# Rotary embedding (NeoX) on one core: joining the f32 heads' transfer, limiting the queued loads, cutting the tables in two

## The chip, the core and the metric

The kernel runs on one core of a Trainium2 chip. The metric is device microseconds of one execution. A profiled execution gives a span, which is about 1.8 us shorter than the device time of the same execution. The TensorE clock is 1.00 in all records; TensorE does nothing here.

On one core "slow" only means over 1.5% above the fastest run of the same kernel. Verdicts use fast runs alone; where I use a slow profile I say so.

## The reference

```python
def reference(x, freqs, positions):            # x: 8 x 8 x 1024 x 64 f32
    half = x.shape[-1] // 2
    angles = np.outer(positions, freqs)
    cos, sin = np.cos(angles), np.sin(angles)
    x_first, x_second = x[:, :, :, :half], x[:, :, :, half:]
    out_first = x_first * cos - x_second * sin
    out_second = x_first * sin + x_second * cos
    return np.concatenate([out_first, out_second], axis=-1)
```

There are 64 heads of 256 KB. Each is read once and written once.

## The kernel before

GpSimd issues the bulk of the traffic, in transfers that convert f32 to bf16 on the way in and bf16 to f32 on the way out. 62 heads go that way, in eight groups; a partition holds 64 positions of one head, 16 KB in HBM and 8 KB in SBUF. Heads 0 and 1 go through SP in f32, so that the DMA engines have work before the first bulk load. VectorE does three operations for each group (product with sine, product with cosine, sum of the first swapped and the second).

```python
    def hbm_head(t, i):
        return bass.AP(tensor=t.tensor, offset=t.offset + i * head, ap=[[R * d, P], [1, R * d]])
    ...
    xf = singles.tile([P, edge, R, d], f32)            # R = 8: 2 KB a partition and head
    for i in range(edge):
        nc.sync.dma_start(out=xf[:, i], in_=hbm_head(x, i))
    nc.scalar.dma_start(out=pos_i..., in_=positions...)
    nc.scalar.dma_start(out=fr[0:P:8], in_=freqs[None, :].to_broadcast([P // 8, half]))
    xts = []
    for lo, n in groups:                               # 6 heads, then seven times 8
        xt = xpool.tile([P, run], bf16, name="xt")[:n * chunks]
        parts = 2 if lo == groups[-1][0] else 1
        for a in range(0, run, run // parts):
            b = a + run // parts
            nc.gpsimd.dma_start(out=xt[:, a:b], in_=hbm(x, lo, n, a, b))
        xts.append(xt)
    ...
    pool.keepalive_nop(ins=[pool.lower_ap(xts[-1][:, :run // 2])])   # stores only after the loads
```

## Time and profile before

| | before |
|---|---|
| device time, first three runs | 86.14 us median (85.05 to 87.10) |
| profiled run | 84.02 us, span 82.1 us |
| all loads landed / all stores landed | 42.1 / 81.2 us |
| VectorE's last operation ends | 76.8 us |

How GpSimd issues its loads, here from the timeline (start, time, instruction, count; in brackets the idle time before it and what ended it):

```profile
1.26 4.37 POOL L82 DMA_DIRECT2D xt<-in_x_dram  x8 [0.82 <-PEq L231]
8.28 0.53 POOL L82 DMA_DIRECT2D xt<-in_x_dram  x1 [2.65 <-DMA xt<-in_x_dram]
40.37 1.05 POOL L184 DMA_DIRECT2D out_dram<-ot  x2 [31.45 <-DMA xt<-in_x_dram]
```

Eight of the nine loads are issued by 5.6 us and the ninth when the first has landed; then GpSimd waits for the loads and begins with the stores. A transfer runs on 16 DMA engines and has landed only when the last has reported its share.

A transfer runs on 16 DMA engines, and each reports its own share; the trace holds the 16 moments for every transfer (no printed view of the profile shows them, and they do not say which engine reported). I give their median, the last (only then has the transfer landed), and the spread from first to last. In the profiled run before, the 16 engines land the first bulk load within 0.41 us of each other, and every later load within 0.41 us too. I call this "in step", and later also a profile in which no engine lands its share of the first load more than 0.5 us behind the median.

### The profile page before, as it was taken

To read this page: it belongs to the slowest core of one execution; us is meant where nothing else is said; L and a number is where in the kernel's file an instruction comes from. 1 tells how busy PE (TensorE), PEld (TensorE's weight loads), DVE (VectorE), ACT (ScalarE), POOL (GpSimd) and SP (SyncE) were. 2 spreads that over 40 slices of the span, in tenths; PEclk is the share of its full clock that TensorE was granted. 3 is DMA by queue.
4 is the path that set the end of the run, shared out by engine and by line. 5 is a ranking of instruction groups with operands and counts; after the bars stand their busy time and mean duration, and the time that the engine had idled before them with its cause. 6 is when DMAs were issued, how large, how long until landed. Compare 5 with 4: busy or idle time off the path is not lost.

```text
span 82.1 us, 157 instructions
## 1 busy us (share of the span) xinstructions
DVE 67.6 (82%) x49; ACT 9.4 (11%) x8; POOL 9.5 (12%) x22
## 2 busy tenths in 40 slices
DVE  0135996399999996999999999999999999999300
ACT  0600003999000007000000000000000000000000
POOL 4970300000000000000340020002002002002000
DMA  1999999999999999999999999999999999999992
GB/s 19 304 225 212 204 232 216 204 224 212 225 213 204 228 216 200 228 202 208 212 417 415 447 423 439 439 399 463 431 415 447 415 455 431 399 455 405 437 379 104
DMA packets 3456, 25.45 MB, mean 310 GB/s; under 512 B 560, under 2 KB 576, under 8 KB 1600
## 3 DMA queue, kind: packets, MB, share of 16 engines
q0 software_dynamic: 2384, 23.86, 95.0%
q1 hardware_dynamic: 864, 1.57, 5.6%
q10 hardware_dynamic: 208, 0.02, 0.3%
HBM read 16.80 MB, written 16.78 MB: 409 GB/s over the span
## 4 chain that ended last, share of the span: by engine, by line
DVE 78%; DMA 7%; ACT 4%; issue 4%; ACTq 1%
DVE t L151 22%; DVE ot L152 21%; DVE ot L154 19%; DMA const<-in_freqs_dram 7%; DVE turnsc L101 3%; DVE turnsc L95 3%; ACT sinc L105 2%; DVE wholec L99 2%; DVE of L168 2%; DVE of L171 1%; DVE last L154 1%; DVE last L152 1%; ACT cosr L109 1%; DVE sinc L106 1%; DVE turnsr L95 1%
## 5 line engine op out<-in xcount | busy, mean ns | idle before, releaser
L151 DVE TENSOR_TENSOR t<-xt,sinc 128x4096 bf16<-128x4096 bf16 (+3 forms) x9 | 18.3, 2046 | 0.0
L154 DVE TENSOR_TENSOR ot<-ot,t 128x4096 bf16<-128x4096 bf16 (+2 forms) x8 | 17.7, 2222 | 0.2
L152 DVE TENSOR_TENSOR ot<-xt,cosc 128x4096 bf16<-128x4096 bf16 (+2 forms) x8 | 17.6, 2216 | 0.0
L184 POOL DMA_DIRECT2D out_dram<-ot x8 | 4.2, 532 | 61.4 <-DMA xt<-in_x_dram 31.5
L82 POOL DMA_DIRECT2D xt<-in_x_dram x9 | 4.9, 573 | 3.5 <-DMA xt<-in_x_dram 2.6
L105 ACT ACTIVATE sinc<-turnsc 128x2048 bf16<-128x2048 f32 x1 | 1.9, 1909 | 10.3 <-DVE turnsc L101 10.3
L106 DVE TENSOR_SCALAR sinc<-sinc 128x2048 bf16<-128x2048 bf16 x1 | 0.7, 693 | 2.0 <-ACT sinc L105 2.0
L95 DVE TENSOR_TENSOR turnsc<-pos_f,fturn 128x2048 f32<-128x2048 f32 x1 | 2.3, 2291 | 0.0
L101 DVE TENSOR_TENSOR turnsc<-turnsc,wholec 128x2048 f32<-128x2048 f32 x1 | 2.3, 2291 | 0.0
L87 DVE LOAD_MASK_SELECT const<-const x1 | 0.0, 14 | 2.7 <-DMA const<-in_positions_dram 2.7
L109 ACT ACTIVATE cosc<-wholec,half_pi 128x2048 bf16<-128x2048 f32 x1 | 2.0, 2002 | 0.1
L88 DVE LOAD_MASK_SELECT const<-const x1 | 0.0, 14 | 2.3 <-DMA const<-in_freqs_dram 2.3
L108 ACT ACTIVATE wholec<-turnsc 128x2048 f32<-128x2048 f32 x1 | 1.9, 1893 | 0.0
L105 ACT ACTIVATE sinr<-turnsr 128x256 bf16<-128x256 f32 x1 | 0.4, 416 | 10.6 <-DVE turnsr L101 10.6
L105 ACT ACT_TABLE_LOAD x1 | 1.3, 1283 | 2.1 <-issue 2.1
L168 DVE TENSOR_TENSOR of<-x,cosr 128x1024 f32<-128x1024 bf16 x1 | 1.2, 1226 | 0.1
L99 DVE TENSOR_SCALAR wholec<-turnsc 128x2048 f32<-128x2048 f32 x1 | 1.2, 1228 | 0.0
L171 DVE TENSOR_TENSOR of<-of,t 128x1024 f32<-128x1024 f32 x1 | 1.2, 1225 | 0.0
L154 DVE TENSOR_TENSOR last<-last,t 128x1024 f32<-128x1024 f32 x1 | 1.2, 1224 | 0.0
L152 DVE TENSOR_TENSOR last<-xt,cosc 128x1024 f32<-128x1024 bf16 x1 | 1.2, 1218 | 0.0
L126 ACT CAST x<-xf 128x1024 bf16<-128x1024 f32 x1 | 1.0, 1028 | 0.0
L115 DVE CAST pos_f<-const 32x64 f32<-32x64 int32 x4 | 0.8, 211 | 0.1
(17 smaller groups left out, 4.7 us busy)
## 6 DMA issues: line engine op xcount, KB each, us to landing
out_dram<-ot POOLq DMA_DIRECT2D x6, 2048.0 KB, 11.1
xt<-in_x_dram POOLq DMA_DIRECT2D x6, 1024.0 KB, 21.8
out_dram<-ot POOLq DMA_DIRECT2D x2, 1536.0 KB, 6.3
xt<-in_x_dram POOLq DMA_DIRECT2D x2, 512.0 KB, 34.3
xt<-in_x_dram POOLq DMA_DIRECT2D x1, 768.0 KB, 6.7
xf<-in_x_dram SPq DMA_DIRECT2D x2, 256.0 KB, 2.9
out_dram<-of SPq DMA_DIRECT2D x2, 256.0 KB, 2.9
out_dram<-last SPq DMA_DIRECT2D x2, 256.0 KB, 4.0
```

The lines of the kernel that those rows point to most:

```text
L82: nc.gpsimd.dma_start(out=xt[:, a:b], in_=hbm(x, lo, n, a, b))
L95: pin(v.tensor_mul(out=turns, in0=pos_f.to_broadcast([P, n, half]), in1=fturn.to_broadcast([P, n, half])))
L99: pin(v.tensor_scalar(out=whole, in0=turns, scalar1=magic, scalar2=magic, op0=Alu.add, op1=Alu.subtract))
L101: pin(v.tensor_sub(out=turns, in0=turns, in1=whole))
L105: nc.scalar.activation(out=sin[:, :, 0], in_=turns, func=Act.Sin, scale=twopi)
L109: nc.scalar.activation(out=cos, in_=whole[:, :, None, :].to_broadcast([P, n, copies, half]), func=Act.Sin, scale=-twopi, bias=half_pi)
L151: pin(v.tensor_mul(out=t.rearrange(flat4), in0=xt, in1=sin_c[:n, lo:hi].rearrange(flat4)))
L152: pin(v.tensor_mul(out=ot, in0=xt.rearrange("p (c two h) -> p c two h", two=2, h=half), in1=cos_c[:n, lo:hi].to_broadcast([n, rows, 2, hal ...
L154: pin(v.tensor_add(out=ot, in0=ot, in1=swap(t)))
L168: pin(v.tensor_mul(out=o, in0=x0, in1=w.to_broadcast(flat)))
L171: pin(v.tensor_add(out=pair, in0=pair, in1=swap(t.rearrange(rows, two=2, h=half))))
L184: tc.keep_in_program_order(pool.dma_start(out=hbm(out, lo, n, 0, hi * d), in_=ot.rearrange(flat4)))
```

## The change

The intent: fewer and larger packets for the f32 heads, no long queue of loads in front of the small transfers, ScalarE and VectorE overlapped while the tables are made.

```diff
-    for i in range(edge):
-        nc.sync.dma_start(out=xf[:, i], in_=hbm_head(x, i))
+    nc.sync.dma_start(out=xf, in_=hbm_first(x))       # R = 16: 128 rows of 4 KB over both heads
...
     for lo, n in groups:
+        if len(xts) >= 2:
+            nc.gpsimd.keepalive_nop(ins=[nc.gpsimd.lower_ap(xts[-2])])
...
-        nc.scalar.activation(out=sin[:, :, 0], in_=turns, func=Act.Sin, scale=twopi)
+        for c in cuts:                                 # two halves for the large tables
+            pin(nc.scalar.activation(out=sin[:, c, 0], in_=turns[:, c], func=Act.Sin, scale=twopi))
...
-    tc.keep_in_program_order(nc.scalar.dma_start(out=pos_r...))
+    for i in range(edge):
+        pin(nc.scalar.dma_start(out=pos_r[i * each:(i + 1) * each]...))
...
-    for i in range(edge):
-        tc.keep_in_program_order(sp.dma_start(out=hbm_head(out, i), in_=of[:, i]))
+    tc.keep_in_program_order(sp.dma_start(out=hbm_first(out), in_=of.rearrange(flat4)))
```

Cut away: the VectorE operations are all pinned in order; the heads' tables are made between a group's cosine product and its sum; the signs of the sine table are set in halves; a small memset moves from GpSimd to VectorE.

More of the change, by code (lines that the diff above doesn't have):

```diff
@@ L36 @@
     C = 64
-    R = seq // P
     chunks = seq // C
@@ L40 @@
     edge = 2
+    R = edge * seq // P
     run = C * d
@@ L43 @@
     groups = [(edge, first)] + [(g, G) for g in range(G, bh, G)]
-    assert chunks * C == seq and G * chunks == P and bh % G == 0 and R * P == seq and chunks <= 32
+    assert chunks * C == seq and G * chunks == P and bh % G == 0 and R * P == edge * seq and chunks <= 32
     singles = ctx.enter_context(tc.tile_pool(name="singles", bufs=1))
@@ L53, in hbm, with hbm_first @@
                        ap=[[run, n * chunks], [1, b - a]])
-    def hbm_head(t, i):
-        return bass.AP(tensor=t.tensor, offset=t.offset + i * head, ap=[[R * d, P], [1, R * d]])
+    def hbm_first(t):
+        return bass.AP(tensor=t.tensor, offset=t.offset, ap=[[R * d, P], [1, R * d]])
     v = nc.vector
@@ L66 @@
     fr = const[:, C * words:].bitcast(f32)
-    xf = singles.tile([P, edge, R, d], f32)
-    for i in range(edge):
-        nc.sync.dma_start(out=xf[:, i], in_=hbm_head(x, i))
+    xf = singles.tile([P, R * d], f32)
+    nc.sync.dma_start(out=xf, in_=hbm_first(x))
     nc.scalar.dma_start(
@@ L73 @@
     nc.scalar.dma_start(out=fr[0:P:8], in_=freqs[None, :].to_broadcast([P // 8, half]))
+    half_pi = singles.tile([P, 1], f32)
+    v.memset(half_pi, math.pi / 2)
     xts = []
     for lo, n in groups:
+        if len(xts) >= 2:
+            nc.gpsimd.keepalive_nop(ins=[nc.gpsimd.lower_ap(xts[-2])])
         xt = xpool.tile([P, run], bf16, name="xt")[:n * chunks]
@@ L81 @@
             b = a + run // parts
-            nc.gpsimd.dma_start(out=xt[:, a:b], in_=hbm(x, lo, n, a, b))
+            tc.keep_in_program_order(nc.gpsimd.dma_start(out=xt[:, a:b], in_=hbm(x, lo, n, a, b)))
         xts.append(xt)
-    half_pi = singles.tile([P, 1], f32)
-    nc.gpsimd.memset(half_pi, math.pi / 2)
     v.stream_shuffle(pos_i, pos_i, [i % chunks for i in range(32)])
-    v.stream_shuffle(fr, fr, [0] * 32)
-    fturn = singles.tile([P, 1, half], f32)
-    v.tensor_scalar_mul(out=fturn[:, 0, :], in0=fr, scalar1=1.0 / twopi)
@@ L92, in tables @@
-    def tables(pos_f, n, copies, name, pin=lambda i: i):
+    pin = tc.keep_in_program_order
+    def tables(pos_f, n, copies, name, parts):
         turns = singles.tile([P, n, half], f32, name=f"turns{name}")
-        pin(v.tensor_mul(out=turns, in0=pos_f.to_broadcast([P, n, half]),
-                         in1=fturn.to_broadcast([P, n, half])))
         whole = singles.tile([P, n, half], f32, name=f"whole{name}")
-        magic = 1.5 * 2.0 ** 23
-        pin(v.tensor_scalar(out=whole, in0=turns, scalar1=magic, scalar2=magic,
-                            op0=Alu.add, op1=Alu.subtract))
-        pin(v.tensor_sub(out=turns, in0=turns, in1=whole))
@@ L103, in tables @@
         sin = singles.tile([P, n, 2, half], bf16, name=f"sin{name}")
         cos = singles.tile([P, n, copies, half], bf16, name=f"cos{name}")
-        nc.scalar.activation(out=sin[:, :, 0], in_=turns, func=Act.Sin, scale=twopi)
+        magic = 1.5 * 2.0 ** 23
+        m = n // parts
+        cuts = [slice(i * m, i * m + m) for i in range(parts)]
+        for c in cuts:
+            shape = [P, m, half]
+            pin(v.tensor_mul(out=turns[:, c], in0=pos_f[:, c].to_broadcast(shape),
+                             in1=fturn.to_broadcast(shape)))
+            pin(v.tensor_scalar(out=whole[:, c], in0=turns[:, c], scalar1=magic, scalar2=magic,
+                                op0=Alu.add, op1=Alu.subtract))
+            pin(v.tensor_sub(out=turns[:, c], in0=turns[:, c], in1=whole[:, c]))
@@ L106, in tables, with negate @@
+        for c in cuts:
+            pin(nc.scalar.activation(out=sin[:, c, 0], in_=turns[:, c], func=Act.Sin, scale=twopi))
+            pin(nc.scalar.activation(out=whole[:, c], in_=turns[:, c], func=Act.Abs))
+            pin(nc.scalar.activation(
+                out=cos[:, c], in_=whole[:, c, None, :].to_broadcast([P, m, copies, half]),
+                func=Act.Sin, scale=-twopi, bias=half_pi))
+        return sin, cos
+    def negate(sin):
         pin(v.tensor_scalar_mul(out=sin[:, :, 1], in0=sin[:, :, 0], scalar1=-1.0))
-        nc.scalar.activation(out=whole, in_=turns, func=Act.Abs)
@@ L109, in tables @@
-        nc.scalar.activation(out=cos, in_=whole[:, :, None, :].to_broadcast([P, n, copies, half]),
-                             func=Act.Sin, scale=-twopi, bias=half_pi)
-        return sin, cos
     pos_f = singles.tile([P, C, 1], f32)
     for q in range(0, P, 32):
-        v.tensor_copy(out=pos_f[q:q + 32],
-                      in_=pos_i.rearrange("p (c w) -> p c w", w=words)[:, :, :1])
-    sin_c, cos_c = tables(pos_f, C, 1, "c")
-    pos_r = singles.tile([P, R, words], i32)
-    tc.keep_in_program_order(nc.scalar.dma_start(
-        out=pos_r.bitcast(positions.dtype),
-        in_=bass.AP(tensor=positions.tensor, offset=positions.offset,
-                    ap=[[R, P], [1, R], [1, 1]])))
@@ L125 @@
-    x0 = singles.tile([P, edge, R * d], bf16)
-    tc.keep_in_program_order(nc.scalar.copy(out=x0, in_=xf.rearrange("p e r d -> p e (r d)")))
+        pin(v.tensor_copy(out=pos_f[q:q + 32],
+                          in_=pos_i.rearrange("p (c w) -> p c w", w=words)[:, :, :1]))
+    pin(v.stream_shuffle(fr, fr, [0] * 32))
+    fturn = singles.tile([P, 1, half], f32)
+    pin(v.tensor_scalar_mul(out=fturn[:, 0, :], in0=fr, scalar1=1.0 / twopi))
+    sin_c, cos_c = tables(pos_f, C, 1, "c", 2)
+    pos_r = singles.tile([P, R, words], i32)
@@ L128, in swap @@
+    each = P // edge
+    for i in range(edge):
+        pin(nc.scalar.dma_start(
+            out=pos_r[i * each:(i + 1) * each].bitcast(positions.dtype),
+            in_=bass.AP(tensor=positions.tensor, offset=positions.offset,
+                        ap=[[R, each], [1, R], [1, 1]])))
+    x0 = singles.tile([P, R * d], bf16)
+    pin(nc.scalar.copy(out=x0, in_=xf))
     def swap(ap):
@@ L132, in swap, with rotate @@
                        ap=[part, rows, [-half, 2], cols])
-    def rotate(xt, n):
-        flat = "p c two h -> p (c two h)"
-        ot = opool.tile([P, C, 2, half], bf16, name="ot")[:n]
-        t = tpool.tile([P, C, 2, half], bf16, name="t")[:n]
-        v.tensor_mul(out=t.rearrange(flat), in0=xt, in1=sin_c[:n].rearrange(flat))
-        v.tensor_mul(out=ot, in0=xt.rearrange("p (c two h) -> p c two h", two=2, h=half),
-                     in1=cos_c[:n].to_broadcast([n, C, 2, half]))
-        v.tensor_add(out=ot, in0=ot, in1=swap(t))
-        return ot
     flat4 = "p c two h -> p (c two h)"
-    def rotate(xt, n, ot, lo, hi, pin):
+    def rotate(xt, n, ot, lo, hi, parts=1, between=None):
         rows = hi - lo
@@ L150, in rotate, with tables_first, rotate_first @@
         t = tpool.tile([P, C, 2, half], bf16, name="t")[:n, :rows]
-        pin(v.tensor_mul(out=t.rearrange(flat4), in0=xt, in1=sin_c[:n, lo:hi].rearrange(flat4)))
+        m = rows // parts
+        for a in range(0, rows, m):
+            if parts > 1:
+                negate(sin_c[:, lo + a:lo + a + m])
+            pin(v.tensor_mul(out=t[:, a:a + m].rearrange(flat4), in0=xt[:, a * d:(a + m) * d],
+                             in1=sin_c[:n, lo + a:lo + a + m].rearrange(flat4)))
         pin(v.tensor_mul(out=ot, in0=xt.rearrange("p (c two h) -> p c two h", two=2, h=half),
                          in1=cos_c[:n, lo:hi].to_broadcast([n, rows, 2, half])))
+        first = between() if between else None
         pin(v.tensor_add(out=ot, in0=ot, in1=swap(t)))
-    def rotate_first():
-        pin = tc.keep_in_program_order
+        return first
+    def tables_first():
         pos_rf = singles.tile([P, R, 1], f32)
         pin(v.tensor_copy(out=pos_rf, in_=pos_r[:, :, :1]))
-        sin_r, cos_r = tables(pos_rf, R, 2, "r", pin)
-        flat = [P, edge, R * d]
-        of = singles.tile(flat, f32)
-        t = tpool.tile([P, C, 2, half], bf16, name="t").rearrange(flat4)
-        t = t[:, :edge * R * d].rearrange("p (n e) -> p n e", n=edge)
-        for o, w in ((t, sin_r), (of, cos_r)):
-            w = w.rearrange("p r two h -> p (r two h)")[:, None, :]
-            pin(v.tensor_mul(out=o, in0=x0, in1=w.to_broadcast(flat)))
-        rows = "p n (r two h) -> p (n r) two h"
-        pair = of.rearrange(rows, two=2, h=half)
-        pin(v.tensor_add(out=pair, in0=pair, in1=swap(t.rearrange(rows, two=2, h=half))))
+        return tables(pos_rf, R, 2, "r", 1)
+    def rotate_first(sin_r, cos_r):
+        negate(sin_r)
+        of = singles.tile([P, R, 2, half], f32)
+        t = tpool.tile([P, C, 2, half], bf16, name="t")[:, :R]
+        for o, w in ((t, sin_r), (of, cos_r)):
+            pin(v.tensor_mul(out=o.rearrange(flat4), in0=x0, in1=w.rearrange(flat4)))
+        pin(v.tensor_add(out=of, in0=of, in1=swap(t)))
         return of
@@ L176 @@
     pool.keepalive_nop(ins=[pool.lower_ap(xts[-1][:, :run // 2])])
-    tail = 2 * R
+    tail = 16
+    piece = tail // 2
     ots = []
@@ L181 @@
         ot = opool.tile([P, C, 2, half], bf16, name="ot")[:n * chunks, :hi]
-        rotate(xt, n * chunks, ot, 0, hi, tc.keep_in_program_order if i > 1 else lambda ins: None)
+        first_tables = rotate(xt, n * chunks, ot, 0, hi, 1 if i else 2, tables_first if i == 1 else None)
         ots.append(ot)
@@ L186 @@
         if i == 1:
-            of = rotate_first()
+            of = rotate_first(*first_tables)
     last = singles.tile([P, tail, 2, half], f32)
-    rotate(xts[-1], P, last, C - tail, C, tc.keep_in_program_order)
+    rotate(xts[-1], P, last, C - tail, C)
     sp = nc.sync
@@ L196 @@
     sp.keepalive_nop(ins=[sp.lower_ap(xts[-1][:, :run // 2])])
-    for i in range(edge):
-        tc.keep_in_program_order(sp.dma_start(out=hbm_head(out, i), in_=of[:, i]))
+    tc.keep_in_program_order(sp.dma_start(out=hbm_first(out), in_=of.rearrange(flat4)))
     for i, done in enumerate(ots[:-1]):
-        sp.clobber_nop(outs=[sp.lower_ap(ap) for ap in [done] + [of[:, j] for j in range(edge) if j == i]])
-    for r in range(0, tail, R):
+        sp.clobber_nop(outs=[sp.lower_ap(ap) for ap in ([done] if i else [done, of])])
+    for r in range(0, tail, piece):
         a = (C - tail + r) * d
-        tc.keep_in_program_order(sp.dma_start(out=hbm(out, groups[-1][0], G, a, a + R * d),
-                                              in_=last[:, r:r + R].rearrange(flat4)))
+        tc.keep_in_program_order(sp.dma_start(out=hbm(out, groups[-1][0], G, a, a + piece * d),
+                                              in_=last[:, r:r + piece].rearrange(flat4)))
     sp.clobber_nop(outs=[sp.lower_ap(ots[-1])])
-    for r in range(0, tail - R, R):
-        sp.clobber_nop(outs=[sp.lower_ap(last[:, r:r + R])])
+    for r in range(0, tail - piece, piece):
+        sp.clobber_nop(outs=[sp.lower_ap(last[:, r:r + piece])])
 _INS = ['x', 'freqs', 'positions']
```

## The prediction

> **What bounds the kernel now.** I read first the page of the kernel before: its busy shares, its forty slices, its queues.
>
> ```profile
> span 82.1 us, 157 instructions
> DVE 67.6 (82%) x49; ACT 9.4 (11%) x8; POOL 9.5 (12%) x22
> ...
> DMA  1999999999999999999999999999999999999992
> GB/s 19 304 225 212 204 232 216 204 224 212 225 213 204 228 216 200 228 202 208 212 417 415 447 423 439 439 399 463 431 415 447 415 455 431 399 455 405 437 379 104
> ...
> q0 software_dynamic: 2384, 23.86, 95.0%
> q1 hardware_dynamic: 864, 1.57, 5.6%
> q10 hardware_dynamic: 208, 0.02, 0.3%
> HBM read 16.80 MB, written 16.78 MB: 409 GB/s over the span
> ```
>
> VectorE is busy 82% of the span, but the DMA row is 9 in every slice except the first and the last, and the three queues' packet times add up to 100.9% of the span. GB/s seems to double at slice 20 (41 us), but does not: the bulk loads convert f32 to bf16 and are counted at the bf16 side, so 212 GB/s of a load is about 424 GB/s read from HBM. Loads run first, stores second: 16.80 MB read from 1.75 us (first slice with traffic, in quarter-microsecond windows) to about 41.4 us is 424 GB/s, 16.78 MB written from there to 80.6 us is 428 GB/s. So one stream of 33.6 MB runs at one rate from 1.75 to 80.6 us.
>
> The chain that ended last names another limit: VectorE for 78%. In order of time, it has these pieces:
>
> ```profile
> 1.51 5.53 DMA const<-in_freqs_dram
> ...
> 11.34 2.30 DVE turnsc L101
> 13.64 0.02 issue
> 13.67 1.92 ACT sinc L105
> 15.59 0.02 issue
> 15.61 0.70 DVE sinc L106
> 16.31 0.02 issue
> 16.34 4.49 DVE t L151 x2
> ...
> 29.63 0.09 DVE pos_rf L160
> ```
>
> VectorE waits for the frequencies, builds the cosine and sine tables, waits 2.0 us for ScalarE's sine, and from 16.34 us works without a pause to 76.79 us. Which limit is real at the end? For that, the timeline (start, duration, instruction) and the two-microsecond windows of the end (last two figures: DMA busy share, GB/s):
>
> ```profile
> 68.93 0.53 POOL L184 DMA_DIRECT2D out_dram<-ot  x1 [6.20 <-DVE ot L154]
> 74.06 0.53 POOL L184 DMA_DIRECT2D out_dram<-ot  x1 [4.60 <-DVE ot L154]
> 76.79 0.81 SPq L203 DMA_DIRECT2D out_dram<-last  x2
> ...
> 76.00:78.00 2.00, 0.76 (x1) 0.00 (x0) 0.00 (x0) 1.00 1.08 430
> 78.00:80.00 2.00, 0.00 (x0) 0.00 (x0) 0.00 (x0) 1.00 0.99 378
> 80.00:82.00 2.00, 0.00 (x0) 0.00 (x0) 0.00 (x0) 1.00 0.31 118
> ```
>
> I worked the store queue forward at 434 GB/s, the mean of the windows from 42 to 76 us. A 2.10 MB store then takes 4.83 us, the two of 1.57 MB 3.62 us each, the f32 heads and the final f32 piece (0.52 MB each) 1.21 us each. When stores start at 41.4 us, the heads and three groups are ready or nearly so: 1.21 + 3.62 + 4.83 + 4.83 = 14.5 us of work, to 55.9 us. The next ends at 60.7, the next (ready 55.5) at 65.6, the next (ready 62.2) at 70.4. The last full one, issued at 68.93, is needed at 70.4 and goes to 75.2; the 1.57 MB one, issued at 74.06, is needed at 75.2 and goes to 78.9; the last piece, issued from 76.79 to 77.6, is needed at 78.9 and ends at 80.1, against 80.6 measured. So every store arrives about 1 us before the DMA engines need it. They are the bound, and VectorE has about 1 us of slack: it costs time if it becomes more than that later, and gives none if it becomes earlier.
>
> **What the Trainium skill says.** "DMA: Bandwidth & Descriptors", section "Bandwidth", gives 435 GB/s as the ceiling of the fabric and 425 GB/s measured for 16 MB; the trace, with 424 and 428, agrees, and leaves no more than 2 to 3% to find. The same page, "Queues, rings and completion order", says that an engine takes turns between queues a packet at a time. The trace agrees: the position table of the f32 heads, 8 KB in total, took 8.7 us from issue to landing beside the bulk loads. "SBUF — State Buffer" says, in its warning on GpSimd-issued DMAs, that a two-port VectorE instruction keeps GpSimd from writing descriptors. In this trace stores issued beside tensor-tensor work cost 532 ns and loads 573 ns, so no such delay shows; the new loads will be issued beside more kinds of instructions. "VectorE: DVE Perf Modes", "Side-by-side", gives 2293, 1224 and 693 ns for 2048 elements at one, two and four a cycle; the rows here say 2291, 1228 and 693 ns, so I size the new shapes by its sum (elements divided by the mode, plus about 150 cycles, at 0.96 GHz).
>
> **The change, part by part.**
>
> *One transfer for both f32 heads, 4 KB a partition.* Bytes stay, 128 packets of the load and 128 of the store go. Queue q1 took 5.6% of 82.1 us on 16 engines, 73.6 us of engine time, for 768 data packets of 2 KB (its 864 less 16 completions for each of six transfers): 95.8 ns each. Bulk queue q0 moved about 32.0 MB at the HBM side in 95.0%, or 78.0 us: 2.44 us a MB, thus 80 ns for 2 KB. The 16 ns between are an estimate of a packet's fixed cost. 256 packets fewer, over 16 engines: 256 x 16 / 16 = 0.26 us. Saved on the bound itself: up to 0.26 us. One SP issue of about 0.4 us less, not on the path.
>
> *Two loads queued.* GpSimd issues load i only once load i-2 has landed. Load i-1, 4.9 us of DMA work, is still queued then, against 0.57 us for an issue and something like 1 us to the first byte. No gap: 0. The engines would have to drift some 3 us apart for one to run dry, and the share stays near 1 at the change to stores, where the issue is gated in the same way. The 2.65 us for which GpSimd waited before its ninth load in the trace of before goes; no one needed it.
>
> *Tables in two halves.* In f32, 1024 elements cost (1024 + 150) / 0.96 = 1.22 us, and in the two-a-cycle scalar operation 0.69. With the frequencies landing at 7.04 us again, the first half is ready at 7.5 + 1.22 + 0.69 + 1.22 + gaps = 10.7, the second at 13.9 us. ScalarE starts at 10.7 instead of 13.67; six operations of about 1.05 us (from 1.9 us for 2048, with some 0.2 fixed) end at about 17.0, with the second sine at 14.9. VectorE: sign 0.42 us to 14.3, first half product 1.22 to 15.5, sign 0.42 to 15.95, second half 1.22 to 17.2, then the cosine product, just ready, to 19.4 and the sum to 21.65. Group 1's two products (2.2 us each) end at 26.05 us, with only that group's sum (2.25 us) still to do; the kernel before had both groups done at 29.63, so this stretch gains 29.63 - 26.05 - 2.25 = 1.3 us.
>
> *Tables of the heads.* Now 512 wide, not 256: 0.69 + 0.42 + 0.69 + 0.1 for positions = 1.9 us against 1.3; the 0.46 us wait for ScalarE is hidden behind group 1's sum. From 26.05: tables 1.9, sum 2.25, sign and three operations 0.3 + 0.69 + 1.23 + 1.23 = 3.45, then the unchanged rest (34.99 to 76.77, 41.8 us): 75.45 us, 1.3 us earlier than 76.79. But the positions now come in two transfers issued at about 17.0 and 17.4 us; at 8.7 us or a little more each, they land between 25.7 and 27, where VectorE wants them at 26.05. That can eat up to 1 us. VectorE's end: 75.4 to 76.4 us. Being inside or ahead of the present slack, this is worth nothing, except that the last pieces mix better with the group store: the 4.55 us after 76 us ran at 407 instead of 434 GB/s, a loss of 0.28 us, of which I give back 0.1.
>
> **Sum:** 0.26 + 0 + 0 + 0.1 = 0.36 us less, 0.4%.
>
> **Rivals.** *VectorE is the bound, as the chain says.* Then the end follows it by 0.4 to 1.3 us and the time is 84.8 to 85.7 us. For it: the chain's 78%. Against: the DMA share of 1.08 in the very window in which VectorE stops. *The throttled loads open gaps.* If engines drift, or descriptors wait behind VectorE's two-port sign and table operations, each of seven gates could cost 0.2 to 0.5 us: 1.4 to 3.5 us, or 87.5 to 89.6 us. For it: the section on GpSimd-issued DMAs; against: operations of that kind last at most 0.7 us beside a queue of several microseconds. *A shorter queue makes all transfers smoother.* The small transfers at the start (5.5 us for 2 KB of frequencies) could land sooner, which only helps VectorE, and the bulk rate could rise to 435 GB/s: 33.6 MB / 435 = 77.2 us against 78.85 now, 1.6 us less, 84.5 us. Nothing in the trace says that a full queue slows the engines.
>
> **Range and chances.** 86.14 - 0.36 = 85.8; I take 85.7, giving the second and third gains a little. The three runs before spread over 2.05 us (85.05 to 87.1), so a median may wander by some 0.8 us whatever the change: 84.5 to 86.8. Over 2% faster means under 84.4, which needs both the smoother stream and a lucky median: 0.11. Slower by 2% means over 87.9, only by gaps: 0.04. Within: 0.85.
>
> **What would show it.** Right: the DMA row still 9 throughout and HBM bytes unchanged; 256 packets fewer in q1 and its share down by about 0.3 points; VectorE's last operation at 75.4 to 76.4 us with the last DMA byte still near 80.2; no group product waiting for a load. Wrong: slices under 9 in the DMA row at 8 to 40 us (gaps of the gate); a VectorE wait for the heads' positions above 1 us; a last byte that moves along with VectorE; or a bulk stream above 430 GB/s at the HBM side, which would make the number too high.

## The result, and the profile after

The changed kernel takes 88.06 us (87.62 to 88.19, four runs) against 85.59 us before (84.24 to 87.10, four runs). The ratio of the fast runs is 1.0395, 95% interval 1.0288 to 1.0502: slower, and outside my range. A ratio is always the mean time of one kernel's fast runs over that of the other's in the same rounds, so it is not quite the ratio of the medians.

The page of the changed kernel, the same rows as in the prediction:

```profile
span 86.2 us, 169 instructions
DVE 68.9 (80%) x55; ACT 10.9 (13%) x11; POOL 9.5 (11%) x21
...
DMA  1999999999999999899999999999999999999990
GB/s 38 308 180 209 217 183 183 202 167 191 206 181 217 186 221 194 179 217 186 213 255 422 441 418 449 434 418 456 411 456 395 456 411 456 403 449 413 433 343 20
...
q0 software_dynamic: 2384, 23.86, 93.6%
q1 hardware_dynamic: 576, 1.57, 5.0%
HBM read 16.80 MB, written 16.78 MB: 390 GB/s over the span
```

The bytes are the same. The DMA row is still almost all nines, which alone would say that nothing changed. The GB/s row tells more: while loads run (up to slice 20 or so) it dips to 167, 181, 186, 179, where before it stayed between 200 and 232. While stores run it is as before. The busy share counts an engine as busy while a packet is under way, however long that packet takes.

The chain in order of time (start, us, what), for the places shown before:

```profile
1.48 6.33 DMA const<-in_freqs_dram
...
17.24 11.07 DMA pos_r<-in_positions_dram
...
28.40 0.19 DVE pos_rf L170
...
76.57 1.22 DVE last L164
```

The heads' positions, issued from 16.7 us on, keep VectorE waiting until 28.4 us. VectorE ends at 77.79 us, 1.0 us later than before, although its tables were made in two halves.

The timeline of GpSimd and of SP's final store:

```profile
1.26 1.19 POOL L85 DMA_DIRECT2D xt<-in_x_dram  x2 [0.82 <-PEq L241]
10.64 0.54 POOL L85 DMA_DIRECT2D xt<-in_x_dram  x1 [8.19 <-DMA xt<-in_x_dram]
15.62 0.69 POOL L85 DMA_DIRECT2D xt<-in_x_dram  x1 [4.44 <-DMA xt<-in_x_dram]
21.00 0.53 POOL L85 DMA_DIRECT2D xt<-in_x_dram  x1 [4.68 <-DMA xt<-in_x_dram]
43.99 1.59 POOL L193 DMA_DIRECT2D out_dram<-ot  x3 [6.81 <-DMA xt<-in_x_dram]
80.16 0.81 SPq L211 DMA_DIRECT2D out_dram<-last  x2
```

The third load is issued at 10.64 us, where the first load's landing let the kernel before issue its ninth at 8.28. The stores start at 43.99 instead of 40.37 us: 3.6 us later. The last store is issued 2.4 us after VectorE is done, because SP first waits for earlier stores to land. And in the windows (last two figures: DMA busy share, GB/s) the rate falls soon after a gated load's issue at a share that hardly falls:

```profile
12.00:14.00 2.00, 1.93 (x3) 1.97 (x3) 0.00 (x0) 1.00 0.93 139
14.00:16.00 2.00, 1.97 (x3) 2.00 (x3) 0.38 (x1) 1.00 1.06 213
18.00:20.00 2.00, 2.00 (x1) 0.94 (x1) 0.00 (x0) 1.00 0.90 156
```

The landings of the 16 engines give the sum (us from the start of the span; "last" is the slowest engine):

```
                      before    changed
first load, median      7.70      7.74
first load, last        8.00     10.07      spread 0.41 -> 2.52
all loads, last        42.14     45.75      +3.61
all stores, last       81.17     84.99      stores take 39.03 -> 39.24
span                   82.1      86.2
```

So 3.6 of the 3.8 us between the last landings were lost while loading, 0.2 while storing. In the first load most engines are on time, but one is 2.3 us behind the median and another about 1.5. From the third load on, the medians of successive loads are 5.2 to 5.7 us apart (the two halves of the last one take 4.9 together); before they were 4.9. Packets of a bulk load took 0.62 to 0.63 us almost without exception before (median and 90th percentile 0.625, longest 0.99). In the changed kernel they take up to 2.2 us, most of all where one load follows another.

### The profile page after: what moved, and what is told of

Its sections match the earlier page's. It is cut to its first block, busy times and chain, and to the rows that moved or that the text cites. A ratio compares the mean times of both kernels' runs of the same rounds, so it can differ in the third digit from the quotient of the medians.

```text
span 86.2 us, 169 instructions
## 1 busy us (share of the span) xinstructions
DVE 68.9 (80%) x55; ACT 10.9 (13%) x11; POOL 9.5 (11%) x21
## 4 chain that ended last, share of the span: by engine, by line
DVE 59%; DMA 20%; ACT 7%; issue 3%; ACTq 0%; DVEq 0%
DVE t L159 16%; DVE ot L164 15%; DVE ot L161 15%; DMA pos_r<-in_positions_dram 13%; DMA const<-in_freqs_dram 7%; ACT sinc L110 2%; ACT wholec L112 2%; ACT cosc L113 2%; DVE turnsc L108 1%; DVE turnsc L104 1%; DVE of L179 1%; DVE last L164 1%; DVE of L178 1%; DVE last L161 1%; DVE wholec L106 1%
## 5 line engine op out<-in xcount | busy, mean ns | idle before, releaser
L110 ACT ACTIVATE sinc<-turnsc 128x1024 bf16<-128x1024 f32 x2 | 2.1, 1058 | 8.2 <-DVE turnsc L108 8.2
L108 DVE TENSOR_TENSOR turnsc<-turnsc,wholec 128x1024 f32<-128x1024 f32 x2 | 2.5, 1225 | 0.1
L104 DVE TENSOR_TENSOR turnsc<-pos_f,fturn 128x1024 f32<-128x1024 f32 x2 | 2.4, 1222 | 0.0
L113 ACT ACTIVATE cosc<-wholec,half_pi 128x1024 bf16<-128x1024 f32 x2 | 2.3, 1150 | 0.1
L110 ACT ACTIVATE sinr<-turnsr 128x512 bf16<-128x512 f32 x1 | 0.6, 630 | 11.6 <-DVE turnsr L108 11.6
L112 ACT ACTIVATE wholec<-turnsc 128x1024 f32<-128x1024 f32 x2 | 2.1, 1042 | 0.0
L106 DVE TENSOR_SCALAR wholec<-turnsc 128x1024 f32<-128x1024 f32 x2 | 1.4, 694 | 0.1
L113 ACT ACTIVATE cosr<-wholer,half_pi 128x1024 bf16<-128x1024 f32 x1 | 1.1, 1150 | 0.0
```

The lines of the kernel that those rows point to most:

```text
L104: pin(v.tensor_mul(out=turns[:, c], in0=pos_f[:, c].to_broadcast(shape), in1=fturn.to_broadcast(shape)))
L106: pin(v.tensor_scalar(out=whole[:, c], in0=turns[:, c], scalar1=magic, scalar2=magic, op0=Alu.add, op1=Alu.subtract))
L108: pin(v.tensor_sub(out=turns[:, c], in0=turns[:, c], in1=whole[:, c]))
L110: pin(nc.scalar.activation(out=sin[:, c, 0], in_=turns[:, c], func=Act.Sin, scale=twopi))
L112: pin(nc.scalar.activation(out=whole[:, c], in_=turns[:, c], func=Act.Abs))
L113: pin(nc.scalar.activation(out=cos[:, c], in_=whole[:, c, None, :].to_broadcast([P, m, copies, half]), func=Act.Sin, scale=-twopi, bias=ha ...
```

## The experiments

Three theories stood at first. **Gate**: the limit of two loads issues each load too late. **Step**: the single heads' transfer puts the engines out of step. **VectorE**: its later end does it. I number the runs as they were made. "Ungated" is the changed kernel without the two lines of the gate.

### e1: the gate taken out

```diff
-        if len(xts) >= 2:
-            nc.gpsimd.keepalive_nop(ins=[nc.gpsimd.lower_ap(xts[-2])])
```

> The changed kernel with all loads queued at once again, nothing else changed. Gate theory (each gated load reaches the DMA engines too late and starts with slow packets): the loads end near 42.7 us again instead of 46.4, the span falls by about 3.5 us, ratio to the kernel before 0.99 to 1.00. Step theory (the single 4 KB transfer of the f32 heads puts the 16 DMA engines out of step at the start and they stay so): still slow, 1.03 to 1.04, with a landing spread of over 2 us in the first load. VectorE theory (its end moved 1.0 us later because of the heads' positions): ratio near 1.01.

Measured: 87.08 us (86.54 to 87.51), ratio 1.030, interval 1.021 to 1.040. The page:

```profile
DMA  1999999999999999999679999999999999999980
GB/s 43 306 182 194 228 201 228 205 224 210 212 228 201 232 197 236 197 205 215 135 290 447 418 441 387 472 402 464 394 472 394 472 394 472 394 472 400 429 311 12
```

The dips during the loads are gone, but at slices 19 and 20 the DMA row shows 6 and 7: most engines are done with loading and idle while the stores wait for an engine that is not. The landings: first load median 7.70, last 10.44, and every later load has its slowest engine about 2.7 us behind its first, until the loads end at 44.57 us (median engine: 41.99). So without the gate the engines keep their pace, and the lag of the first load is carried unchanged to the turn from loads to stores. Against before that is 44.57 - 42.14 = 2.43 us; the gate adds 45.75 - 44.57 = 1.18 us. Both theories have a part and neither is the whole.

### e2: three loads queued instead of two

```diff
-        if len(xts) >= 2:  ... xts[-2]
+        if len(xts) >= 3:  ... xts[-3]
```

> The changed kernel with three loads kept queued instead of two. Gate theory: each gated load is issued a whole load (4.9 us) earlier, so the slow first packets go or nearly go: ratio to the kernel before 0.99 to 1.01. Step theory: no change, 1.03 to 1.04.

Measured: 87.17 us (86.82 to 87.39), ratio 1.031. It is the ungated kernel over again: first load spread 3.04 us, loads 4.9 us apart, end of loads 44.99 us. One more load in the queue takes the gate's cost away and leaves the lag.

### e3: the heads in two transfers of 2 KB packets, with the gate

```diff
-    nc.sync.dma_start(out=xf, in_=hbm_first(x))
+    for i in range(2):      # every row of 4 KB cut in two halves
+        nc.sync.dma_start(out=xf[:, i * 512:(i + 1) * 512], in_=...)
```

> The changed kernel with the f32 heads loaded in two transfers of 2 KB a partition, the gate kept. Gate theory: no gain, 1.03 to 1.04. Step theory: the first load lands with a spread under 0.5 us as before and the ratio falls to 1.00 to 1.01.

Measured: 88.07 us (87.84 to 88.50), ratio 1.0425. The first load's spread is 2.19 us. Packets of 2 KB do not cure it.

### e4: the kernel before with the gate alone

```diff
+        if len(xts) >= 2:
+            nc.gpsimd.keepalive_nop(ins=[nc.gpsimd.lower_ap(xts[-2])])
```

Cut away: the loads are pinned in program order, and GpSimd's small memset moves ahead of them.

> The kernel before with the gate of two loads alone. Gate theory: 1.03 to 1.04, the loads ending some 3.5 us later. Step theory: 1.00, since its f32 transfers are the old ones.

Measured: 84.41, 87.51, 87.52 and 88.57 us; one fast run, so there is no ratio, and the profile (88.57) is slow. With the gate, the one good run is as good as the kernel before. The slow profile has a first load spread of 3.07 us with the old f32 transfers. So the lag exists without the heads' change, in some runs. The runs of the kernel before in these rounds say the same: 84.25 to 84.63 in four, 85.58, and 86.27 to 86.74 in four. What I had taken for a noisy median is two ways of running.

### e5: the heads' part alone, on the kernel before

```diff
-    for i in range(edge):
-        nc.sync.dma_start(out=xf[:, i], in_=hbm_head(x, i))
+    nc.sync.dma_start(out=xf, in_=hbm_first(x))      # and the store, the positions and R likewise
```

No gate, the old tables and order.

> The kernel before with the heads' part alone: one transfer of 4 KB a partition each way, no gate, the old tables and order. In the runs so far the kernel before shows two times, about 84.4 us (all 16 engines land each load within 0.4 us of each other) and about 86.5 us; the ungated changed kernel always showed about 87 us, with one or two engines 2 to 3 us behind from the first load on (call it a straggler). Heads theory (the single 4 KB load makes the straggler the rule): all four times 86.3 to 87.5, spread of the first load over 2 us. Rival (the rest of the changed order does it, or chance): the same mix of 84.4 and 86.5 as before.

Measured: 86.90 us (85.88, 86.53, 87.27, 87.51); the ratio of its two fast runs is 1.015, interval 1.008 to 1.022. First load spread 1.80 us. One run and the spread are a little under what I had expected, but no run is near 84.5, where six of the nine runs of before in these rounds were between 84.50 and 85.16. This profile has a second loss: the frequencies land late (VectorE starts on them at 8.76 us, before at 7.07), VectorE ends at 79.98 us, and the stores take 39.76 us instead of 39.03. So here, unlike in e7, a late VectorE may have cost up to 0.7 us.

### e6: the tables and the order alone

The ungated changed kernel with the heads loaded and stored as before:

```diff
-    nc.sync.dma_start(out=xf, in_=hbm_first(x))
+    for i in range(edge):
+        nc.sync.dma_start(out=xf[:, i], in_=hbm_head(x, i))      # store, positions and R likewise
```

> The changed kernel without the gate and with the heads as before (two transfers of 2 KB a partition each way): only the tables in halves and the fixed VectorE order are left. Heads theory: the mix of 84.4 and 86.5 us of the kernel before, or better. Rival (tables and order make the straggler the rule): all times 86.3 to 87.5. VectorE's own time must not matter in either: its end 0.5 to 1.3 us earlier than before, no gain from it.

Measured: 83.95, 84.01, 84.06, 84.29, and 86.69, 87.02 us. The ratio of the fast runs is 0.989, interval 0.986 to 0.992. So this part of the change is harmless or worth about 1%; I had put it at 0.1 us. The profile, of one of the two slow runs (86.69), has the lag, a spread of 2.91 us. Because there is no in-step profile of this kernel, I cannot say where its 0.9 us come from. Nor do later rounds confirm them: e9 and e12 below have the same tables and order, and the ratio of their fast runs is 0.997 in both, with intervals from 0.988 to 1.006; and the kernel before itself ran at 84.07 to 84.46 us in seven of eleven runs of later rounds (those of e13) on a chip with the same number.

### e7: the frequencies issued before the heads, ungated

```diff
+    nc.sync.dma_start(out=fr[0:P:8], in_=freqs...)
     nc.sync.dma_start(out=xf, in_=hbm_first(x))
-    nc.scalar.dma_start(out=fr[0:P:8], in_=freqs...)
```

> The changed kernel, ungated, with the frequencies issued by SP ahead of the heads, so that their small packets do not fall into the first bulk load. If these packets set the straggler off: in-step engines (first load spread under 0.5 us) and 84 to 85 us. If the heads' transfer does it: no change, about 87 us.

Measured: 86.65 us (85.30 to 86.92), spread 2.39 us, so these small packets are not what sets the lag off. It has a second use. VectorE ends at 74.59 us here and at 76.48 us in e1, but the two profiled runs take 86.51 and 86.54 us and their last bytes land at 83.55 and 83.57 us. Moving VectorE by 1.9 us moved the end by nothing: the VectorE theory is out for the changed kernel.

### e8: the heads' load only after the first bulk load, ungated

```diff
-    nc.sync.dma_start(out=xf, in_=hbm_first(x))
 ... after the loop over the groups:
+    nc.sync.keepalive_nop(ins=[nc.sync.lower_ap(xts[0])])
+    tc.keep_in_program_order(nc.sync.dma_start(out=xf, in_=hbm_first(x)))
```

> The changed kernel, ungated, with the heads' load issued only when the first bulk load has landed. If the overlap of the heads' load with the start of the bulk load sets the straggler off: first load spread under 0.5 us; the DMA engines lose up to 1.9 us at the start, where they now have nothing to do before the bulk load, so 85.5 to 87 us. If not: straggler as before and 88 to 89 us.

Measured: 85.25, 85.36, 85.41, 85.60 us, ratio 1.0055, first load spread 0.78 us. The same single transfer of 4 KB packets, moved away from the start of the bulk load, does no harm beyond the time in which the engines have less to do at the start. In none of these four runs, without the overlap of the two at the start, does the lag appear (the spread is over the 0.5 us that I had set, but no engine is more than 0.4 us behind the median).

### e9: one transfer, 2 KB packets, heads laid out as before

```diff
 (against e6)
-    for i in range(edge):
-        nc.sync.dma_start(out=xf[:, i], in_=hbm_head(x, i))
+    nc.sync.dma_start(out=xf..., in_=...)     # ap=[[R * d, P], [head, edge], [1, R * d]]
```

> The order-only kernel (no gate, heads laid out as before) with its two head loads joined into one transfer that still moves 2 KB a packet. So far: with 2 KB per-head loads some runs are in step (84 us) and some have the straggler (86.5 to 87 us); with the 4 KB layout no run of an ungated kernel was under 85.3. If issuing one transfer instead of two (all packets ready about 0.4 us sooner) is what makes the straggler the rule: no run near 84, median 86.5 to 87. If the 4 KB layout is: the same mix as the order-only kernel, with runs near 84.

Measured: 84.56, 84.57, 84.95, 86.63, 86.99, 87.48 us. The mix of the kernel before; so issuing one transfer instead of two is not it.

### e10: two transfers of 64 partitions, 4 KB packets, ungated

```diff
-    nc.sync.dma_start(out=xf, in_=hbm_first(x))
+    for i in range(2):
+        nc.sync.dma_start(out=xf[i * 64:(i + 1) * 64], in_=...)   # head i
```

> The ungated changed kernel with the heads loaded in two transfers of 64 partitions, still 4 KB a packet. If 4 KB packets make the straggler the rule: 86 to 87.5 in every run. If the single issue does: runs near 84.3 appear in about half.

Measured: 84.73 to 85.61 us in six runs, median 84.87, ratio 0.999, first load spread 0.72 us. The packets are the ones of the changed kernel, every byte goes to the same place, and the lag is gone in these six runs (e16 repeats them). So 4 KB packets alone are not the cause either.

### e11: two transfers of 2 KB packets that take every other 2 KB, ungated

This is e3 without the gate:

```diff
 (against e3)
-        if len(xts) >= 2:
-            nc.gpsimd.keepalive_nop(ins=[nc.gpsimd.lower_ap(xts[-2])])
```

> The ungated changed kernel with the heads loaded in two transfers of 2 KB packets that take every other 2 KB of HBM (the first such run had the gate too and showed nothing of this). If packet size makes the straggler the rule: runs near 84.3 appear. If it is the layout in HBM, or the layout only changes the odds by chance: 86 to 87.5 in every run.

Measured: 86.56 us (85.91 to 86.88), ratio 1.0175, spread 2.47 us. Packet size is ruled out from this side too.

### e12: the second head's load held back, on e6's kernel

```diff
 (against e6)
-    for i in range(edge):
-        nc.sync.dma_start(out=xf[:, i], in_=hbm_head(x, i))
+    nc.sync.dma_start(out=xf[:, 0], in_=hbm_head(x, 0))
 ... after the loop over the groups:
+    nc.sync.keepalive_nop(ins=[nc.sync.lower_ap(xts[0])])
+    tc.keep_in_program_order(nc.sync.dma_start(out=xf[:, 1], in_=hbm_head(x, 1)))
```

> The order-only kernel, with the second head's load held back until the first bulk load has landed, so that the heads' traffic is nearly done when the bulk starts. If the overlap of the two sets off the straggler: every run between 84.2 and 85.0, first load spread under 0.8 us; 0.98 to 1.00 of before. If any heads' transfer at the start can do it: some runs at 86.5 to 87.

Measured: 84.41, 84.44, 85.50, 85.69, 86.55, 86.57 us. The profile (85.69, slow) has a spread of 1.82 us. A miss: one head alone at the start is enough to leave an engine behind sometimes.

Here the cause of the lag and the price of the gate were still open.

### e13 and e17: one transfer, partitions alternating between the two heads, ungated

```diff
-        ap=[[R * d, P], [1, R * d]]
+        ap=[[R * d, P // edge], [head, edge], [1, R * d]]
```

The positions (now one transfer) and the store of the heads follow the same order.

> Ungated changed kernel, heads in one transfer of 4 KB packets over 128 partitions, but the partitions alternate between the two heads[...]. If one transfer over 128 partitions is what leaves an engine behind: 86 to 87.5 us in every run. If it is the layout in HBM[...]: runs at 84.5 to 85.6.

> e13 once more. If the mixed layout keeps the engines in step: every run at 84.3 to 85.0. If e13 was chance: some at 86 and above.

Measured: 84.42 to 84.57 us in four runs (ratio 1.001), and 84.50 to 85.02 us in six on another chip (median 84.82, ratio 1.005, while the kernel before had 84.09 to 88.27, median 85.16). First load spreads 0.55 and 0.46 us. The page of e17:

```profile
DMA  0999999999999999999999999999999999999992
GB/s 0 301 207 194 230 210 206 238 194 226 214 205 230 210 214 222 206 202 218 210 416 404 428 451 412 443 420 435 443 412 443 420 451 428 428 443 402 428 383 78
```

No hole at the turn to the stores at slice 20, no dips. It is again one transfer over 128 partitions with 4 KB packets.

### e14: two transfers of 64 partitions, each over both heads, ungated

```diff
-    nc.sync.dma_start(out=xf, in_=hbm_first(x))
+    for i in range(2):       # every other row of 4 KB: ap=[[2 * R * d, 64], [1, R * d]]
+        nc.sync.dma_start(out=xf[i * 64:(i + 1) * 64], in_=hbm_first(x, i))
```

> Ungated changed kernel, heads in two transfers of 64 partitions as in e10, but each takes every other 4 KB row of both heads. If the two transfers of 64 partitions are what keeps the engines in step: 84.5 to 85.6 in every run. If it is that each transfer reads one head: 86 to 87.5.

Measured: 86.00 to 86.73 us, ratio 1.023. By time it looks like the lag, but the profile (86.28) has a first load spread of 0.89 us and all loads landed at 43.08 us, as in step. Its loss is in the stores: from there to the last landing 40.51 us, against 39.03 before. This kernel also stores the heads in two transfers of 64 partitions and fetches their positions in four, which I had not meant to test; what they do to the stores I leave open. For the question it was made for, it says that reading both heads at once is not enough to cause the lag.

### e15: the changed kernel, gate and all, with e10's two transfers

The diff of e10, on the changed kernel with its gate.

> The changed kernel, gate of two loads and all, with only the heads' load split into two transfers of 64 partitions. If the gate costs only by waiting for an engine that is behind (landing, 0.56 us to the issue and 2.3 us to the first packet make 2.9 us, against 4.87 us of a load still queued): in step, no gap, 84.7 to 85.6 as e10. If the gate costs by itself: 85.7 to 87, with load landings more than 4.9 us apart.

Measured: 84.78, 85.08, 85.78 and 90.01 us; ratio of the fast runs 1.010, interval 1.003 to 1.016. In the profile (85.78, fast) the spread is 1.00 us, the loads are 4.6 to 5.05 us apart, and they end at 43.03 us, against 42.69 in e10. With engines in step the same gate costs 0.34 us of loading, not 1.18. The stores of this profile also take 0.72 us longer than in e10 (39.79 against 39.07), for which I have no explanation; but over all, the three fast runs average 85.21 us, against 84.93 for the five in-step runs of the same kernel without the gate in the same rounds (e16), so about 0.3 us stand. The run of 90.01 us was not profiled and is not explained.

### e16: e10 once more

No edit.

> e10 once more. Nothing new if it holds: every run within 84.5 to 85.6, where the kernel before has some at 86 and above. If e10 was chance: some runs at 86 to 87.5.

Measured: 84.80 to 85.15 us in five runs, 86.51 and 87.02 in two. The profile is of the slow kind and has the lag (spread 2.35 us). So the split of e10 makes the lag rare, not impossible.

### e18: e13 with the frequencies first

The diff of e7, on e13's kernel.

> e13 with the frequencies issued by SP ahead of the heads, as in e7, which lets VectorE end about 1.9 us earlier. If the DMA engines are the bound: within 0.3 us of e17. If VectorE is part of the bound once they are in step: 1 us or more faster. If the change at the start puts an engine behind: 86 and above.

Measured: 84.49 to 84.85 us, ratio 1.004. But VectorE ended at 75.9 us, as in e17 (75.8), so this run does not answer what it was made for; e7 against e1 remains the evidence on VectorE. As six more runs of the alternating layout it counts.

### All runs by the form of the heads' load

Runs above 86.0 us, as a rough count of those with the lag; only one run of each kernel was profiled, so the lag of the others is inferred from their time. It is rough because the gate adds to the time (changed, e2, e3, e4, e15), because e12's profile at 85.69 us has a lag too, and because e14, left out here, is slow for another reason:

```
heads' load at the start of the kernel                     kernels              above 86
two transfers of 2 KB, one per head                        before               18 of 55
two transfers of 2 KB, one per head                        e6                    2 of 6
two transfers of 2 KB, one per head, gated                 e4                    3 of 4
one transfer of 2 KB packets, one per head inside          e9                    3 of 6
one transfer of 2 KB, first head only                      e12                   2 of 6
one transfer of 4 KB, row p to partition p                 changed,e1,e2,e5,e7  18 of 20
two transfers of 2 KB, every other 2 KB                    e3,e11                9 of 10
two transfers of 64 partitions, 4 KB                       e10,e15,e16           3 of 17
one transfer of 4 KB, partitions alternate between heads   e13,e17,e18           0 of 16
none at the start                                          e8                    0 of 4
```

The forms were not all run in the same rounds, or on the same chip; the kernel before was in every round, and had runs above 86 in each (18 of 55 together).

The profiles with the lag also show two pictures of it. Counting the engines that land their share of the first load more than 1 us behind the median, it is one engine with the old form, with one head alone, and in e16's slow run (e4, e6, e12, e16: 2.66, 2.63, 1.59 and 2.11 us behind), but two to five where one transfer, or two of every other 2 KB, cover both heads row by row (changed 2, e1 2, e2 4, e3 5, e5 5, e7 3, e11 5). So it may be more than one effect.

## Why the prediction was wrong, point by point

**"They are the bound, and VectorE has about 1 us of slack."** The bound held; the whole loss is in the DMA stream, and e7 against e1 shows VectorE off the path. My slack was drawn from an ideal queue, though, and I had overlooked that SP issues the last store only after the earlier ones have landed.

**"Saved on the bound itself: up to 0.26 us."** The packets behave as worked out. Queue q1 went from 864 to 576 packets (256 of data, 32 of completions), and its time from 5.6% of 82.1 us, 4.60 us, to 5.0% of 86.2 us, 4.31 us: 0.29 us less, a little above the 0.26. But the term stands for only a part of what this change does. I priced the heads' transfer by its bytes and packets and never asked what it does to the load that starts beside it. What the runs showed in its place: in this form it leaves two to five of the 16 engines more than 1 us behind in every profile (the slowest 1.3 to 2.9 us), and by the times in nearly every run (18 of 20), where the old form did in a third of them (18 of 55). In the ungated kernels an engine that is behind stays behind (e1: 2.7 us from the first load to the last), so no other takes over its work, and the stores wait for the last load. This is the first step that failed. Against the in-step profile of the kernel before it is worth +2.43 us (44.57 against 42.14 us for the end of the loads); against the in-step kernels of the new order, whose loads end at 42.69 (e10), 42.68 (e13) and 42.71 us (e17), about 1.9 us, and the other 0.5 us is not explained.

**"No gap: 0. The engines would have to drift some 3 us apart for one to run dry."** This is the second. I had the right condition and assumed it away: they drifted 2.5 us in the first load. A gate on a landing waits for the slowest engine; the landing came at 10.07 us, the issue at 10.64, and most engines finished the load still queued at about 12.7 us. Packets that start from 12.1 us on took up to 2.0 us instead of 0.62. Worth +1.18 us (changed against e1), and 0.34 us when the engines are in step (e15 against e10). My "something like 1 us to the first byte" was not read from the trace: there the first load took 2.31 us from the start of its issue to its first packet (1.26 to 3.57). By the sum the new packets come about when the queued load runs out, neither clearly early nor late, so why the first packets of a gated load take so long is not shown. e8 gives a hint: there the first bulk load has hardly anything beside it, and its packets that start before 4 us still take 1.27 us at the median, against 0.62 in the kernel before. A load that is not queued behind another may simply start slowly.

**"VectorE's end: 75.4 to 76.4 us."** It was 77.79. The frequencies landed 0.8 us later than I assumed, and the positions cost 1.49 us where I had allowed "up to 1 us". With no effect on the time, as far as e7 against e1 shows. (That VectorE works "without a pause" from 16.34 us was read too quickly, too: it waits 0.46 us for ScalarE at the heads' tables, as the prediction itself says further down.)

**"Tables in two halves ... worth nothing."** Nearly. e6 puts tables and order at 0.9 us in its fast runs, where I gave 0.1; e9 and e12 do not confirm it. If any part of the change is a gain, it is this one.

**The rivals.** "The throttled loads open gaps", 87.5 to 89.6 us, contains the result, and I had given "slower" 0.04. Of its two reasons the first was right, engines that drift; the second was not, descriptors that wait behind VectorE: the gated loads took 0.53 to 0.69 us to issue, as others do. It counts seven gates where the changed kernel has six. "VectorE is the bound" is out.

**The signs.** Two of my four signs of being wrong came: a slice under 9 between 8 and 40 us (slice 16 of the DMA row, an 8), and a wait for the heads' positions above 1 us (1.49). Of the signs of being right, the bytes and the 256 data packets fewer in q1 came too, so those say nothing on the loss.

**The range.** I called the spread of the first three runs, 85.05 to 87.10, a wandering median. It is two ways of running, and a change can alter the odds between them. The trace before me was one of the good way.

**What stays open.** Why the lag arises at all, and which property of the heads' transfer sets its odds. No run without the overlap at the start had it (e8, four runs). It is not the packet size (e10, e11), not the single issue (e9, e13), not the frequencies' packets (e7). The layout, or the timing that comes with it, matters: e13 and the ungated changed kernel differ in the order in which the partitions take their rows, and in their small position transfers at 17 us, after the lag has set in. But the traces differ in time as well: the heads' first packet starts at 1.76 us in e1 and at 2.18 in e13, the first bulk packet at 3.19 and 3.81. No run separates this rival from the layout. The length of the overlap is not it: in e10 the heads' packets run beside the bulk load until 8.1 us with the engines in step, in e1 only until 3.7. The Trainium skill, "DMA: Bandwidth & Descriptors", section "The descriptor swizzle", would put partitions 0 to 63, thus all of head 0, on eight engines and head 1 on the other eight in the changed kernel, and both on each engine in e13; no run here shows the assignment. But e14 reads both heads at once and was in step, so this is no explanation yet.

No kernel of mine beats the one before clearly at its best: e6 does by 1.1% in the fast runs of its own rounds, but not beside later runs of before, and it has slow ones. What e13 and e17 offer is steadiness: none of their ten runs is slow, and their medians (84.47 and 84.82 us) stand beside 84.34 and 85.16 for all runs of the kernel before in the same rounds.

## What to carry to other kernels

Where DMA is the bound, look at when each of the 16 engines lands its share of a transfer, not only at the busy row: that stays at nine while packets take three times as long. A wait for a landing is a wait for the slowest engine, so a limit on queued transfers should leave room for the drift as well as for the issue (here three queued loads cost nothing that the times show, 87.17 against 87.08 us, while two cost 1.2 us with the lag and about 0.3 without). And before a spread of a few runs is taken for noise, see whether its times fall into two groups, and which of them the profile belongs to.

## What the Trainium skill lacked or had wrong

- "DMA: Bandwidth & Descriptors" says that the engines of a transfer finish independently, and that two of them (7 and 15) are usually the slower ones, but not by how much engines can part or that they stay parted: within 0.41 us in every load of the good profile, 2.7 us from the first load to the last in e1. (The landings here carry no engine number, so whether 7 and 15 are the ones behind can't be said; in e2, e3, e5, e7 and e11 it is more than two.) Nor does it have that a transfer on a second queue beside the start of a bulk load can leave engines 1 to 3 us behind, with odds that depend on how that transfer is cut (18 of 20 runs above 86 us against 0 of 16).
- The same page's table of specifications gives about 1 us to the first byte for transfers issued by GpSimd. Here the first packet came 1.35 us after the start of the issue with only the small transfers on the way (e8: 1.26 to 2.61 us), but 1.9 to 2.3 us beside the heads' load (e1: 1.26 to 3.19 us; before: 1.26 to 3.57). I found no page that has what a wait for a landing adds: about 0.56 us from the last engine to the next issue with the gate (10.07 to 10.64 us), and 0.28 us where the transfer itself waits, without the gate's own instruction (before: 8.00 to 8.28 us).
